# The gate of the pooling branch as a stage of its own by seven products

## The chip, the cores and the metric

The kernel runs on one core of one Trainium2 chip. The metric is the device time of one execution in microseconds. A core has a matrix engine (PE, with its weight loads shown as PEld), VectorE (DVE), ScalarE (ACT), GpSimd (POOL) and SyncE (SP, which here only issues transfers). Each engine takes its own instructions in order; they wait for one another by semaphores. PE writes its sums to eight banks of 512 floats per partition; here they are four tags ("pj", "z", "av", "tr") of two banks.

## The reference

One layer of a decoder block on a sequence of 1024 rows of width 1024, all in 32-bit floats. The input x is normed and modulated to h, and one projection of h gives eight parts of 1024 columns each:

```
h = rms_norm(x, norm_gain) * (1 + scale) + shift
q, k, v, z_a, u, z_b, m_a, m_b = split(h @ w_in)
attn   = stick_breaking(q, k, v)        # 16 heads of 64; A[t,s] = sigmoid(z_ts) * prod_{s<j<t} (1 - sigmoid(z_tj)), s < t
p_a    = (attn * silu(z_a)) @ w_branch_a
pooled = trailing-window means of u (2, 4, 8, 16) minus u, a linear map per group, a scale per channel
p_b    = (pooled * silu(z_b)) @ w_branch_b
merged = sigmoid(m_a) * p_a + sigmoid(m_b) * p_b
out    = final rms_norm(x + gate * (merged @ w_out))
```

The two joining gates are sigmoid(m_a) for the attention and sigmoid(m_b) for the pooling branch. Each comes from one 1024 x 1024 x 1024 product of h.

## The kernel before, in words

**Arithmetic.** A 32-bit operand is split into a high part (ScalarE rounds it, an fp32r number) and a low part (the rest, one subtraction on VectorE or GpSimd). A product takes three matmuls: high by high, high by low, low by high. So a tile of 128 columns of a projection, over eight blocks of 128 and two halves of the sequence, takes 48 matmuls of 128x512. h is held transposed, as `hT` (high and low), in SBUF. Time runs backwards along the sequence, which only matters to the order of rows.

**Stages, as us from the start of the span in the profile before.** Up to 128 the start (norm, `hT`, the weights of u with the pooling maps folded in, u). From 128 to 205 the values, from 205 to 300 the projection z_b with the pooling's window sums on VectorE, from 300 to 369 the branch p_b, from 369 to 1011 the attention, and to 1192 the finish (p_a and out).

**Seven products.** The values and p_b are computed by `seven` (L565): both 1024-wide operands are cut into four 512-blocks, sums and differences of blocks are formed (of the weights on VectorE as they are loaded, L576 to L588; of h once, in four tiles `ht0` to `ht3`, the list `tq`), and seven block products p1, p5, p6, p7, p4, p3, p2 of 48 matmuls each give the four blocks of the result: 336 matmuls in place of 384. Operands are loaded in halves ("quarters" of an operand, q = 0 and 1) by `raw`: the first of a pair goes to one of two buffers `raw`, the second to one of two buffers `ar`. `a_op` and `b_op` (L546, L552) make high and low parts of the two sides, on ScalarE and VectorE. After a product, `copied` (L598) takes sums out of PE's banks on ScalarE, `added` (L562) adds chains on VectorE, and `final` hands a finished 128x512 block to the caller: `values` rounds it (L683, ScalarE), subtracts (L684, VectorE) and stores both parts in `v_d` (L685, SP's queue). These stages keep all weight loads and these stores on the one queue of SP, in program order.

**Attention.** The heads are done in eight pairs, each pair in eight units of 256 query rows (`HT_ORDER`). For a unit: PE forms the scores z (L898 on), ScalarE the two sigmoids `om` and `be` (L907, L908), GpSimd masks the diagonal block (L912), VectorE scans `om` along the keys (L914) and multiplies `be` by it (L915). Then, a chunk of two key blocks at a time, PE transposes `be` into a bank (`wt`, tag "tr"), ScalarE rounds it (L933), VectorE subtracts the low part (L934) and PE multiplies by the values (`av`). Scores run three units ahead of the products (`LEAD`), turned chunks two ahead (`DEPTH`).

**The filler.** Between these pieces, PE is given quanta of three matmuls of the projections that are left: per pair the keys, the queries and the attention's gate z_a, and among them the tiles of the two joining gates, 40 tiles of 48 matmuls, 640 quanta. 62 quanta run ahead (`FIRST`), `QUANTA` = 70 in each pair, the remaining 18 behind the last pair. `GATES` says how many joining-gate tiles follow each pair's keys and queries; tiles left over go to the end. Keys and queries of a pair are projected during the pair before, made into high and low parts (`kh`, `klo`, `q`, `qlo`) and copied across partitions by transfers (`kh<-kh`). A filler tile's weights are loaded by SP (L129), rounded by ScalarE (L121) and subtracted by GpSimd (L116; one of the 40 by VectorE). A joining gate's half goes through a sigmoid on ScalarE (L167) and is stored from ScalarE's queue (L168) to `sa_d` or `sb_d`, which the finish reads back (L1074, L1076).

**What sets the order.** In the attention, PE's order is pinned to the order in which the program is written (`order`, L97); elsewhere, and on the other engines, a scheduler decides by its own estimate of when things are ready. On VectorE the multiplication by the scan is issued behind the next low part (`behind`, `flush`).

The functions that the change touches:

## Time and profile before

| what | value |
|---|---|
| median of 3 runs | 1191.57 us (1191.53 to 1192.69) |
| the profiled execution | 1194.0 us, its span 1192.3 us |
| mean granted clock of PE | 0.998 |
| PE busy | 1179.2 us (99%), 5650 instructions |
| VectorE busy | 826.6 us (69%) |
| ScalarE busy | 542.3 us (45%) |
| GpSimd busy | 255.1 us (21%) |
| attention, 369 to 1011 us | PE 639.1, VectorE 461.1, ScalarE 351.0, GpSimd 238.2 us |
| values, 128.4 to 205 us | PE 76.6, VectorE 49.9, ScalarE 36.6 us |
| matmuls of filler (p<-hT,w) | 1920 |

The span runs from the first to the last instruction of the profiled execution; the time of a run holds a little more than the span. A line of the timeline gives the start, the duration, the engine, the line, what is written and read, and in brackets the idle time before and what ended it; "SPq" and "ACTq" are the issuing of transfers by these engines. Busy time is an average over stages: what a change in one stage is worth is read in that stage.

### The profile page before, as it was taken

The numbers are of one execution on the slowest core, as the hardware profiler recorded it, in microseconds if no ns is written. First come the engines' busy times: TensorE is split into PE (matmuls) and PEld (weight loads), VectorE is DVE, ScalarE is ACT, GpSimd is POOL, SyncE is SP. The second block draws the span as 40 slices with busy tenths as digits, with TensorE's granted clock in tenths as the row PEclk, the third lists the DMA queues.
The fourth block names the chain that finished last, engine by engine and source line by source line (L and its number), as shares of the span: only waits on it lengthen the run. The fifth ranks groups of instructions, "written<-read, shape, count | busy, mean of one in ns | idle before, by whom it ended". The sixth has DMA issues, their size and how long they took to land.

```text
span 1192.3 us, 15804 instructions
## 1 busy us (share of the span) xinstructions
PE 1179.2 (99%) x5650; PEld 984.6 (83%) x5650; DVE 826.6 (69%) x1093; ACT 542.3 (45%) x1016; POOL 255.1 (21%) x384
## 2 busy tenths in 40 slices
PE   8999999999999999999999999999999999999997
PEld 7888888888888788888888888888888888888886
DVE  5767466698762577877778687786877853885643
ACT  5561354322541555556556565555555643232111
POOL 1000000000003233244333344333434431000001
PEclk9999999999999999999999999999999999999999
DMA  9652329653457331422415224152321224974612
GB/s 349 259 187 98 131 91 318 229 192 89 142 175 237 92 98 46 136 84 89 106 47 137 85 85 100 56 137 76 113 78 58 71 102 177 346 267 160 228 54 88
DMA packets 73312, 167.26 MB, mean 140 GB/s; under 512 B 9233, under 2 KB 22673, under 8 KB 71058
## 3 DMA queue, kind: packets, MB, share of 16 engines
q1 hardware_dynamic: 65026, 151.38, 39.2%
q10 hardware_dynamic: 8208, 14.88, 3.4%
q8 instruction: 44, 0.72, 0.3%
q14 instruction: 34, 0.28, 0.1%
HBM read 115.89 MB, written 33.56 MB: 125 GB/s over the span
## 4 chain that ended last, share of the span: by engine, by line
PE 82%; DVE 7%; DMA 5%; issue 4%; POOL 1%; ACT 1%; SPq 1%; POOLq 0%; ACTq 0%; DVEq 0%
PE p L101 33%; PE pa L101 7%; PE o L101 6%; PE vp L101 6%; PE z L101 5%; PE av L101 5%; PE wt L101 5%; PE u L101 5%; PE bp L101 4%; PE ua L101 3%; DMA u<-u_d 2%; PE wm L101 1%; DVE om L914 1%; DMA kh<-kh 1%; DVE gb L716 1%
## 5 line engine op out<-in xcount | busy, mean ns | idle before, releaser
L101 PE MATMUL p<-hT,w 128*128 128x512 f32 x1920 | 479.9, 391 | 0.0
L101 PEld LDWEIGHTS p<-hT,w 128*128 128x128 f32 x1920 | 355.2, 188 | 73.9 <-DVE klo L101 0.2
L914 DVE TENSOR_TENSOR_SCAN om<-om 128x512 f32<-128x512 f32 (+7 forms) x128 | 191.2, 1494 | 85.0 <-ACT om L907 51.9
L116 POOL TENSOR_TENSOR w<-w_raw,w 128x1024 fp32r<-128x1024 f32 x39 | 97.2, 2491 | 414.7 <-ACT w L121 409.7
L907 ACT ACTIVATE om<-z 128x512 f32<-128x512 f32 (+2 forms) x192 | 94.6, 493 | 157.1 <-PE z L101 134.6
L934 DVE TENSOR_TENSOR wt<-wt,wt 128x512 fp32r<-128x512 f32 (+1 forms) x160 | 99.4, 621 | 39.4 <-ACT wt L933 38.7
L912 POOL TENSOR_SCALAR_AFFINE_SELECT om<-om 128x128 f32<-128x128 f32 x128 | 72.7, 568 | 205.2 <-ACT om L907 201.8
L933 ACT CAST wt<-wt 128x512 fp32r<-128x512 f32 (+1 forms) x160 | 88.0, 550 | 49.4 <-PE wt L101 49.0
L101 PE MATMUL av<-wt,vv 128*128 128x512 f32 x320 | 106.3, 413 | 0.0
L101 DVE TENSOR_TENSOR be<-be,om 128x511 f32<-128x511 f32 (+7 forms) x128 | 101.1, 794 | 2.0 <-POOL be L912 0.7
L908 ACT ACTIVATE be<-z 128x512 f32<-128x512 f32 (+2 forms) x192 | 94.0, 490 | 0.0
L101 PE MATMUL wt<-ident,be 128*128 128x128 f32 x576 | 89.8, 273 | 1.8 <-DVE wt L934 1.8
L101 PE MATMUL pa<-ga,wa 128*128 128x512 f32 x384 | 89.6, 389 | 0.1
L101 PE MATMUL o<-wo,mhl 128*128 128x512 f32 (+1 forms) x408 | 89.6, 377 | 0.0
L101 PE MATMUL wzb<-hT,wzb 128*128 128x512 f32 x384 | 87.2, 389 | 0.0
L101 PEld LDWEIGHTS o<-wo,mhl 128*128 128x128 f32 x408 | 73.5, 188 | 14.1
L101 PEld LDWEIGHTS pa<-ga,wa 128*128 128x128 f32 x384 | 72.0, 188 | 15.4 <-DVE wa L116 0.5
L101 PEld LDWEIGHTS wzb<-hT,wzb 128*128 128x128 f32 x384 | 72.1, 188 | 14.9
L101 PEld LDWEIGHTS wt<-ident,be 128*128 128x128 f32 x576 | 69.8, 140 | 15.0 <-DVE wt L934 2.5
L101 PE MATMUL z<-kl,q 128*128 128x512 f32 (+2 forms) x192 | 65.5, 341 | 0.0
L101 PE MATMUL z<-kh,q 128*128 128x512 f32 (+2 forms) x192 | 64.0, 334 | 1.1 <-DMA q<-qlo 1.1
L101 PE MATMUL u<-hT,wg 128*128 128x512 f32 x240 | 55.5, 391 | 0.0
(217 smaller groups left out, 1482.0 us busy)
## 6 DMA issues: line engine op xcount, KB each, us to landing
w_raw<-in_w_in SPq DMA_DIRECT2D x40, 512.0 KB, 3.5
v_d<-vo SPq DMA_DIRECT2D x16, 512.0 KB, 4.1
vv<-v_d SPq DMA_DIRECT2D x8, 1024.0 KB, 5.6
wa_raw<-in_w_branch_a SPq DMA_DIRECT2D x16, 512.0 KB, 4.3
wa<-in_w_mod SPq DMA_DIRECT2D x7, 1024.0 KB, 7.5
kh<-kh SPq DMA_DIRECT2D x48, 128.0 KB, 2.3
va<-in_w_v SPq DMA_DIRECT2D x10, 512.0 KB, 3.6
ba<-in_w_branch_b SPq DMA_DIRECT2D x10, 512.0 KB, 4.2
```

What stands on the lines that cost most here:

```text
L101: ins = op(*args, **kw)
L116: lo_eng.tensor_tensor(lo, src, hi.bitcast(F32), op=ALU.subtract)
L716: v.scalar_tensor_tensor(z, dhls[j][:, sh * 512:sh * 512 + 512], psc_v[:, j:j + 1], z, ALU.mult, ALU.mult)
L907: act.activation(om[:, b0:b0 + n], zp[:, :n], AF.Sigmoid, scale=-0.125)
L908: act.activation(be[:, b0:b0 + n], zp[:, :n], AF.Sigmoid, scale=0.125)
L912: gp.affine_select(out=tl[:, :P], in_=tl[:, :P], pattern=[[1, P]], compare_op=ALU.is_gt, fill=fill, base=0, channel_multiplier=-1)
L914: v.tensor_tensor_scan(om[:, :W], om[:, :W], om[:, :W], 1.0, ALU.mult, ALU.min)
L933: act.copy(wt[:, 0, :off], pt[:, :off])
L934: v.tensor_sub(wt[:, 1, :off], pt[:, :off], wt[:, 0, :off].bitcast(F32))
```

## The change

The eight tiles of m_b leave the filler. They are computed by `seven("m", ...)`, behind the values and ahead of z_b, from the same four sums of h (`tq`), whose high and low parts are made again, and from the weights in blocks (`w_mb`, a copy of those columns of `w_in`, laid out like the values' weights). A finished block goes through the sigmoid on ScalarE into one of three buffers and is stored by SP (`gate_b`). The filler has 32 tiles, 512 quanta: 62 ahead, `QUANTA` = 55 in each pair, 10 behind. `GATES` now places one tile of m_a in every second pair; the other four stay for the end. The banks take turns differently: "av", "tr" for the chain b of the new stage, and the branch p_b has its two sets of banks exchanged, with z_b's turns starting afresh. `direct` says that the fourth block may be handed over in PE's bank; it had been tied to `a_moves`.

```diff
-QUANTA = (70,) * 8
-GATES = (0, 1, 2, 1, 2, 1, 1, 2)
+QUANTA = (55,) * 8
+GATES = (0, 1, 0, 1, 0, 1, 0, 1)
...
-    turns = [cycle(("av", "tr", "pj", "z")), cycle(("pj", "z", "av", "tr"))]
+    turns = [cycle(("av", "tr", "pj", "z"))]
...
-    gates = [c + j for j in range(KB) for c in (CMA, CMB)]
+    gates = [CMA + j for j in range(KB)]
...
-    def seven(nm, sums, load, b_of, a_moves, ta, tb, final):
+    def seven(nm, sums, load, b_of, a_moves, ta, tb, final, direct):
...
-                    final(1, 0, j, ps[j] if a_moves else copied("s3", 4, j + 4, ps[j]))
+                    final(1, 0, j, ps[j] if direct else copied("s3", 4, j + 4, ps[j]))
...
+        def h_parts(nm, pl):
+            def of(name, q):
                 if name in ("p1", "p2", "p3"):
                     k, n = dict(p1=(0, 0), p2=(1, 0), p3=(1, 1))[name]
                     return lambda m, e: hT[:, m, 4 * k + 2 * q + e, 512 * n:512 * n + 512]
+                return b_op(k2(tq[("p5", "p6", "p7", "p4").index(name)], q), pl, 2, f"{nm}{name}b{q}")
+            return of
...
-            seven("v", vs, load_v_w, h_parts, True, ("av", "tr"), ("pj", "z"), values)
-    turns.pop(0)
+            seven("v", vs, load_v_w, h_parts("v", vs), True, ("av", "tr"), ("pj", "z"), values, True)
+        with pool("ms", side="right") as ms:
+            def load_m_w(t, m, k, q):
+                nc.sync.dma_start(t.rearrange("p k c -> p (k c)"), a["w_mb"][m, 2 * k + q])
+            def gate_b(m, n, j, src):
+                t = ms.tile([P, 512], F32, tag="go", bufs=3, name=f"sb{4 * m + j}_{n}")
+                act.activation(t, src, AF.Sigmoid)
+                nc.sync.dma_start(sb_d[4 * m + j][:, 512 * n:512 * n + 512], t)
+            seven("m", ms, load_m_w, h_parts("m", ms), False, ("pj", "z"), ("av", "tr"), gate_b, True)
+    turns[0] = cycle(("av", "tr", "pj", "z"))
...
-    seven("b", sums, load_b_w, g_parts, False, ("pj", "z"), ("av", "tr"), branch)
+    seven("b", sums, load_b_w, g_parts, False, ("av", "tr"), ("pj", "z"), branch, False)
...
-            gates = [(c + j, j, d_) for j in range(KB) for c, d_ in ((CMA, sa_d), (CMB, sb_d))]
+            gates = [(CMA + j, j, sa_d) for j in range(KB)]
```

The diff doesn't show three places of the order. First SP's queue at the end of the values in the kernel before (`v_d<-vo` are the stores of finished values; `u`, `sg`, `gbias` and `wzb3_raw` belong to what follows them):

```order
L685 DMA v_d_75<-vo1_0_1633 128x4x256
L129 DMA wzb3_raw_1897<-in_w_in 128x1024
L685 DMA v_d_75<-vo2_0_1638 128x4x256
L685 DMA v_d_75<-vo3_0_1643 128x4x256
L703 DMA gbias_1659<-in_b_gate 128x8
L526 DMA u0_1662<-u_d_78 128x1024
L725 DMA sg_1661<-in_c_row 128x1024
```

In the changed kernel (`ma21`, `ma22`, `ma11s` are the new stage's blocks of weights for p5, the last number before the underscore is the half):

```order
L687 DMA v_d_75<-vo1_0_1633 128x4x256
L697 DMA ma21_1_1764<-in_w_mb 128x1024
L687 DMA v_d_75<-vo2_0_1638 128x4x256
L687 DMA v_d_75<-vo3_0_1643 128x4x256
L697 DMA ma22_0_1728<-in_w_mb 128x1024
L697 DMA ma11s_0_1731<-in_w_mb 128x1024
L697 DMA ma22_1_1766<-in_w_mb 128x1024
L697 DMA ma11s_1_1769<-in_w_mb 128x1024
```

The second operands of p5 stand directly behind the last two stores of values. ScalarE's order at the same place, in the changed kernel (`ms1` is a sum of p1 copied out of its bank, `mp5b` and `mp5a` the high parts of the two sides of p5):

```order
L685 CAST vo3_0_1643<-vs1_3_1157 128x8x64
L598 COPY ms1_0_1714<-mp1_0_1652 128x512
L554 CAST mp5b0_1737<-ht0_832 128x1024
L554 CAST mp5b1_1775<-ht0_832 128x1024
L598 COPY ms1_1_1716<-mp1_1_1653 128x512
L598 COPY ms1_2_1718<-mp1_2_1654 128x512
L598 COPY ms1_3_1720<-mp1_3_1655 128x512
L548 CAST mp5a0_1734<-ma21_0_1726 128x1024
```

All four copies of p1's sums stand ahead of the first high part of p5's left side. The kernel before has here the high parts of z_b's weights and z_b's activations (L715).

Then PE in the attention, at the turn from pair 5 to pair 6. The names are: `p30` and `p15` filler (the number is the tile), `z6_...` scores of pair 6, `wt5_...` and `wt6_...` turned chunks, `av5_...` products with the values; x9 stands for nine matmuls. Before:

```order
L101 MATMUL av5_1_1_7675<-wt5_1_1_1_7552,vv_5_6798 128x2x128
L101 MATMUL p15_0_7684<-hT_91,w15_29_7508 128x512 x9
L101 MATMUL wt5_1_3_3_7694<-ident_79,be5_1_6_7477 128x128 x2
L101 MATMUL wt5_1_3_3_7694<-ident_79,be5_1_7_7537 128x128
L101 MATMUL av5_1_1_7675<-wt5_1_1_2_7619,vv_5_6798 128x512 x2
L101 MATMUL p15_0_7684<-hT_91,w15_29_7508 128x512 x9
L101 MATMUL z6_0_5_0_7714<-kh_6_6971,q0_6_7138 128x384
L101 MATMUL z6_0_5_0_7714<-kl0_2829,q0_6_7138 128x384
L101 MATMUL wt6_0_0_0_7724<-ident_79,be6_0_0_7572 128x128 x2
```

The same place in the changed kernel:

```order
L101 MATMUL av5_1_1_7897<-wt5_1_1_1_7773,vv_5_7145 128x2x128
L101 MATMUL p30_1_7868<-hT_91,w30_23_7552 128x512 x6
L101 MATMUL wt5_1_3_3_7906<-ident_79,be5_1_6_7707 128x128 x2
L101 MATMUL wt5_1_3_3_7906<-ident_79,be5_1_7_7758 128x128
L101 MATMUL av5_1_1_7897<-wt5_1_1_2_7843,vv_5_7145 128x512 x2
L101 MATMUL p30_1_7868<-hT_91,w30_23_7552 128x512 x6
L101 MATMUL z6_0_5_0_7923<-kh_6_7325,q0_6_7555 128x384
L101 MATMUL z6_0_5_0_7923<-kl0_3376,q0_6_7555 128x384
L101 MATMUL wt6_0_0_0_7933<-ident_79,be6_0_0_7802 128x128 x2
```

The turned chunks and the scores keep their order; between them six filler matmuls stand where nine stood, and elsewhere three where six stood.

More of the change, by code (lines that the diff above doesn't have):

```diff
@@ L666, in block_kernel @@
         early.close()
+        def h_parts(nm, pl):
+            def of(name, q):
+                if name in ("p1", "p2", "p3"):
+                    k, n = dict(p1=(0, 0), p2=(1, 0), p3=(1, 1))[name]
+                    return lambda m, e: hT[:, m, 4 * k + 2 * q + e, 512 * n:512 * n + 512]
+                return b_op(k2(tq[("p5", "p6", "p7", "p4").index(name)], q), pl, 2, f"{nm}{name}b{q}")
+            return of
         with pool("vs", side="right") as vs:
@@ L671, in load_v_w @@
                 nc.sync.dma_start(t.rearrange("p k c -> p (k c)"), a["w_v"][m, 2 * k + q])
-            def h_parts(name, q):
-                if name in ("p1", "p2", "p3"):
-                    k, n = dict(p1=(0, 0), p2=(1, 0), p3=(1, 1))[name]
-                    return lambda m, e: hT[:, m, 4 * k + 2 * q + e, 512 * n:512 * n + 512]
-                return b_op(k2(tq[("p5", "p6", "p7", "p4").index(name)], q), vs, 2, f"v{name}b{q}")
             def values(m, n, j, src):
@@ L1159 @@
     w_v = np.asarray(w_in)[0][:, 2 * D:3 * D].reshape(4, 2, P, 2, 512).transpose(3, 0, 2, 1, 4)
+    w_mb = np.asarray(w_in)[0][:, CMB * P:CMB * P + D].reshape(4, 2, P, 2, 512).transpose(3, 0, 2, 1, 4)
     w_ut = np.asarray(w_in)[0][:, CU * P:CU * P + D].reshape(2, 512, 4, 2, P).transpose(2, 0, 4, 3, 1)
@@ L1178 @@
         "w_v": np.ascontiguousarray(w_v).reshape(2, 4, P, D),
+        "w_mb": np.ascontiguousarray(w_mb).reshape(2, 4, P, D),
         "pool_w": np.ascontiguousarray(np.asarray(pool_w)[0]),
```

## The prediction

> **What bounds the kernel now.** I read the page's engine totals first, then PE's waits, then the windows by stage, then the chain of waits. In the windows the columns are PE, PEld, DVE, ACT and POOL busy (with instruction counts), the granted clock, the DMA share and GB/s.
>
> ```profile
> PE 1179.2 (99%) x5650; PEld 984.6 (83%) x5650; DVE 826.6 (69%) x1093; ACT 542.3 (45%) x1016; POOL 255.1 (21%) x384
> ...
> PE wt L101 <- DVE wt L934: 1.8, 4, 0.5
> ...
> 128.40:205.00 76.60, 76.60 (x340) 63.45 (x339) 49.85 (x54) 36.55 (x49) 0.00 (x0) 1.00 0.58 188
> 369.00:1011.00 642.00, 639.08 (x3201) 536.38 (x3200) 461.10 (x603) 350.99 (x736) 238.24 (x330) 1.00 0.33 98
> ...
> 128.48 74.36 PE vp L101 x328
> 992.86 18.39 PE p L101 x81
> ```
>
> PE is busy for 1179.2 of 1192.3 us, and in the whole attention (369 to 1011) it waits for another engine four times, for VectorE's low part of a turned block, 1.8 us in all. So the time is the number of matmuls times their interval, as long as nothing else becomes late. The chain gives the interval: 74.36 / 328 = 0.2267 us in the seven products of the values, 18.39 / 81 = 0.2270 in the filler. The granted clock is 1.00 in both stretches.
>
> **The matmuls removed: −10.9 us.** The gate was 8 tiles of 48 = 384 matmuls of filler; as seven products of 48 it is 336 in a stage of its own. Both kinds are 128x512 at 0.2267: the attention loses 384 × 0.2267 = 87.1, the new stage adds 76.2. Of 640 quanta (three matmuls each) 512 remain: 62 ahead of the turns, 8 × 55 inside the pairs (8 × 70 before), 10 behind the last (18 before). This term holds only where PE keeps its pace; the next three ask where it doesn't.
>
> **The new stage's second product: +2.3 us (1.5 to 4).** The values' own stage ran 76.60 of 76.60 us, with VectorE at 49.85 and ScalarE at 36.55, so the same seven products on the same sums should run without a gap once fed. The question is the feeding at the join.
>
> ```profile
> 193.60 11.04 PE L101 MATMUL vp<-vp2a,hT 128*128 128x512 f32 x48
> 204.48 27.82 PE L101 MATMUL wzb<-hT,wzb 128*128 128x512 f32 x122
> ...
> 208.21 0.62 ACT L683 CAST vo<-vs 128x512 fp32r<-128x512 f32 x1 [1.91 <-DMA v_d<-vo]
> ...
> 208.86 0.69 DVE L684 TENSOR_TENSOR vo<-vs,vo 128x512 fp32r<-128x512 f32 x1 [1.17 <-ACT vo L683]
> ...
> 207.72 2.22 SPq L685 DMA_DIRECT2D v_d<-vo  x2
> ...
> 210.97 1.19 SPq L526 DMA_DIRECT2D u<-u_d  x1
> ...
> va<-in_w_v SPq DMA_DIRECT2D x10, 512.0 KB, 3.6
> ba<-in_w_branch_b SPq DMA_DIRECT2D x10, 512.0 KB, 4.2
> ...
> L598 ACT COPY vs<-vp 128x512 f32<-128x512 f32 x12 | 7.1, 589 | 8.1 <-PE vp L101 8.0
> L548 ACT CAST vp5a<-va 128x1024 fp32r<-128x1024 f32 x2 | 2.1, 1051 | 0.0
> ```
>
> The values' last product ends at 204.48; call it T. The last value row is rounded by ScalarE at 208.21 (it waited for a store to free its buffer) and subtracted at 208.86, and SP is held with its last two stores until 207.72 + 2.22 = 209.94 = T + 5.5. In the changed order the loads of a22 and a11, the first operands of the new p5, stand on SP right behind these two stores. They land 3.6 to 4.2 later, at T + 9.1 to 9.7; the add takes 1.25, so p5's left operand exists at T + 10.4 to 11. ScalarE's copy of p1's fourth sum now stands ahead of its rounding: p1 ends at T + 48 × 0.2267 = T + 10.9, then copy 0.59 and cast 1.05: p5 begins no earlier than T + 12.5, 1.6 after p1, and 1.2 more where it waits for the low part. That gives 1.6 to 2.8. The second half of p5's operands shares two buffers with the first and is loaded once the first add has freed one: T + 11 plus 4.2 for the load, 1.25, 1.05 and 1.2 for add, cast and low part is T + 18.7, and the first half's 24 matmuls end at T + 13.2 + 5.4 = T + 18.6. In the stage of the branch the same wait cost nothing, since its add came 1.6 after p5's start:
>
> ```profile
> 302.52 11.15 PE L101 MATMUL bp<-p5b,bp5a 128*128 128x512 f32 x48
> ...
> 304.14 1.23 DVE L576 TENSOR_TENSOR ba<-ba,ba 128x1024 f32<-128x1024 f32 x1 [2.01 <-DMA ba<-in_w_branch_b]
> ```
>
> So 1.5 to 4; I take 2.3, near the lower sum, because the low part is only the third matmul's operand and the second half comes about even. The stage's stores go onto SP's queue behind its loads: all loads but the last two products' are issued before the first store, and 18 loads of 512 KB in 76 us is what the values had (DMA share 0.58 there), so I cost them at nothing; if that cover failed, the next stage's operands would come late by one store's hold of SP, about 1.1 each.
>
> **Attention with less filler: +6.6 us (0 to 27).** This is the term that decides. A pair's filler falls from 210 to 165 matmuls, 10.2 us less PE work per pair, while VectorE's scans and low parts per pair stay. I cut out, in each pair from the second, the stretch in which VectorE has least room: from the start of a pair's first long scan to the low part of the turned block that PE needs before the second head's first row (chunk 1,0,2):
>
> ```profile
> 466.83:512.58 45.75, 45.32 (x232) 37.93 (x230) 40.05 (x47) 26.67 (x55) 16.46 (x23) 1.00 0.40 110
> 540.99:585.74 44.75, 44.75 (x230) 37.52 (x228) 39.07 (x47) 25.88 (x54) 20.04 (x23) 1.00 0.37 104
> 613.46:658.28 44.82, 44.82 (x228) 37.68 (x227) 40.44 (x48) 27.04 (x55) 16.13 (x23) 1.00 0.35 95
> 687.04:733.73 46.69, 46.69 (x238) 39.26 (x237) 41.12 (x47) 28.30 (x58) 20.39 (x25) 1.00 0.34 99
> 760.68:804.39 43.71, 43.71 (x222) 36.70 (x222) 38.78 (x47) 25.25 (x52) 16.95 (x23) 1.00 0.38 106
> 832.93:880.56 47.63, 46.80 (x236) 38.87 (x235) 40.89 (x47) 28.01 (x57) 19.31 (x25) 1.00 0.38 106
> 907.18:952.28 45.10, 45.02 (x228) 37.63 (x227) 38.44 (x44) 26.94 (x55) 19.84 (x23) 1.00 0.19 65
> sum 318.45, PE 317.11 PEld 265.59 DVE 278.78 ACT 188.08 POOL 129.12; mean PE 45.30 PEld 37.94 DVE 39.83 ACT 26.87 POOL 18.45
> ...
> 514.51 0.49 PE L101 MATMUL wt<-ident,be 128*128 128x128 f32 x3
> ...
> 954.51 0.49 PE L101 MATMUL wt<-ident,be 128*128 128x128 f32 x3
> ```
>
> Over seven stretches the mean is 318.45 / 7 = 45.5 long, VectorE busy 39.8 and idle 5.7. PE takes up the bank that the low part frees somewhat later; in the first and the last of the seven (the two rows of PE) 514.51 − 512.58 = 1.9 and 954.51 − 952.28 = 2.2, and the mean of the seven is 1.7. So PE has 47.2. In the order this stretch holds 138 filler matmuls before and 108 now: 30 × 0.2267 = 6.8 less, 40.4 left. VectorE's own work in it falls a little, since fewer weights' low parts run on GpSimd beside its scans:
>
> ```profile
> 489.58 2.40 POOL L116 TENSOR_TENSOR w<-w_raw,w 128x1024 fp32r<-128x1024 f32 x1 [2.09 <-ACT w L121]
> 489.99 3.87 DVE L914 TENSOR_TENSOR_SCAN om<-om 128x896 f32<-128x896 f32 x1
> ...
> 637.11 2.02 DVE L914 TENSOR_TENSOR_SCAN om<-om 128x896 f32<-128x896 f32 x1
> ```
>
> The same scan takes 2.02 alone and 3.87 beside a low part, 1.85 more. 38 such low parts fall into 642 us, 2.7 per stretch; of 30 some 2.1 will, so at most 0.6 × 1.85 = 1.1 less, and 0.2 for a klo or qlo that slides out: 38.5. That leaves 40.4 − 38.5 = 1.9 for VectorE's idle time where 5.7 stood. What of the 5.7 stays decides: all of it, (5.7 − 1.9) × 7 = 26.6; half, (2.85 − 1.9) × 7 = 6.6; a third or less, 0. What ends it, over the attention:
>
> ```profile
> L914 DVE TENSOR_TENSOR_SCAN om<-om 128x512 f32<-128x512 f32 (+7 forms) x128 | 191.2, 1494 | 85.0 <-ACT om L907 51.9 <-POOL om L912 31.6 <-issue 0.5
> L934 DVE TENSOR_TENSOR wt<-wt,wt 128x512 fp32r<-128x512 f32 (+1 forms) x160 | 99.4, 621 | 39.4 <-ACT wt L933 38.7
> ```
>
> Of 85.0 + 39.4 = 124.4 the 51.9 follow PE's scores, which now come earlier; the 31.6 and 38.7, 57%, are the length of a chain (mask, cast), which a VectorE that comes late finds partly done. I take half.
>
> In the Trainium skill, "SBUF — State Buffer", section "SBUF: two separate sides", VectorE and GpSimd share one port pair that is an exclusive lock for the whole instruction. The trace agrees: the scan beside the low part ended 1.9 us after it (493.86 against 491.98), its own length alone. Taken at its fullest, each of the eight low parts that leave had blocked VectorE for all its 2.40, once a pair instead of my 0.6 times 1.85; VectorE would need 37.2, and with half its idle time the stall would be nil.
>
> Two further deadlines. The keys and queries of the next pair are ready 6 quanta or more of PE work ahead where they were 18 or more, a margin that still covers ScalarE, VectorE and the 2.3 us of the copies; I cost it at nothing, and at 3 us a pair if a copy queues on SP. A filler tile has more time for its weights, (642.0 − 87.1) / 32 = 17.3 us against 642.0 / 40 = 16.1, so their supply is free.
>
> **The tail: +1.2 us (0 to 3).** Behind the last pair 30 filler matmuls remain where 54 of the 81 below stood, 5.4 us less cover for what the finish waits for:
>
> ```profile
> 992.70 18.55 PE L101 MATMUL p<-hT,w 128*128 128x512 f32 x81
> ...
> 1002.57 0.62 ACT L873 CAST ga<-gr 128x512 fp32r<-128x512 f32 x1 [7.01 <-DMA gr<-ga_d]
> ...
> 1003.59 1.04 ACT L121 CAST wa<-wa_raw 128x1024 fp32r<-128x1024 f32 x1
> ...
> 1004.66 1.23 DVE L116 TENSOR_TENSOR wa<-wa_raw,wa 128x1024 fp32r<-128x1024 f32 x1 [0.74 <-ACT wa L121]
> ...
> 1011.09 2.20 PE L101 MATMUL pa<-ga,wa 128*128 128x512 f32 x9
> ```
>
> The last pair's output goes to memory and back, its last cast starts 1002.57, the first finish weight is ready 1004.63 (high) and 1005.89 (low), and PE uses it at 1011.09: 5.2 to 6.5 of room. PE now arrives 5.4 earlier, so between 0.2 of room and 0.2 short by the high part, and a further 1 if ScalarE's remaining gate sigmoids stand before that cast; 1.2.
>
> **Sum:** −10.9 + 2.3 + 6.6 + 1.2 = −0.8. The profiled execution took 1194.0 us (span 1192.3), so 1193.2 for one like it; the median of the runs, 1191.57, is 2.4 shorter at the same work, and against it the sum gives 1190.8.
>
> **Rivals.**
>
> *The idle time gives way (faster).* If VectorE, once late, finds its inputs ready, the 5.7 us shrink to 1.9 and PE keeps its pace through the attention. Only the join and the tail are paid: −10.9 + 2.3 + 1.2 = −7.4, 1184.2. For it: PE waited 1.8 us in 642 so far, and the whole pair leaves room, VectorE's 461.1 / 8 = 57.6 a pair against PE's 62.5 (642.0 less the 62 quanta ahead, 42.2, and the 18.4 behind, by 8 is 72.7, less 10.2). Against it: in the stretch itself 38.5 of 40.4 is 95% busy, and VectorE's order is the scheduler's, with single waits that the average hides.
>
> *VectorE becomes the bound of the stretch (slower).* If 4.2 of the 5.7 us stay, since most of it is the chain from transposes over ScalarE's cast, each of the seven stretches ends (4.2 − 1.9) = 2.3 late, 16.1 in all: −7.4 + 16.1 = +8.7, 1200.3; with all of it kept 1210.8. It decides from the point where −7.4 is used up, 7.4 / 7 = 1.06 a stretch, an idle time of 2.95 us. For it: the four waits that PE has already are all of this kind, and the filler shrinks just where turned chunks follow each other, from nine matmuls to six. Against it: VectorE is busy in 39.83 / 45.5 = 88% of the stretch now, and each turned chunk had room enough for PE not to wait.
>
> *The new stage starves at its start.* If SP is held longer by the value stores, or the second half's loads come a further 4 us late, p5 costs 6 to 8 in place of 2.3 and, with the rest as forecast, the time is about 1195.5. For it: SP's next load behind the last two stores went out 6.5 us after T. Against it: the next product on PE is 10.9 us away from that point, and in the branch's stage a second half's add that came 1.6 after p5's start cost nothing.
>
> On this the Trainium skill, "TensorE: Matmul & The Clock Gate", section "Why this matters for your kernels", warns that a gap of PE above about 3 us brings its clock down to half. No run here shows such a gap between 128 and 1011 us (the granted clock is 1.00 in both windows above); an estimate from that page's window of about 3.4 us at half clock is 1.7 us more for this rival, 1197.2.
>
> **How the numbers follow.** A measurement of this kernel tells about 0.2%, 2.4 us, from no change: faster is below 1189.2, slower above 1194.0. The forecast (half the idle time stays, 1190.8, its own range 1186.5 to 1195.5) has 0.40: 0.27 of it inside the band, 0.08 below, 0.05 above. The idle time giving way has 0.31, all of it faster. VectorE as the bound has 0.21, all of it slower. The starved start has 0.08: 0.04 inside the band, 0.04 above. Faster 0.39, same 0.31, slower 0.30. The range takes in the second case down to a join of 1.5 and a tail of nothing (−10.9 + 1.5 = −9.4, 1182.2, cut to 1182.5) and the third up to 1201.
>
> **What would show it.** Right: no PE gap but one of 1.5 to 4 us before the new stage's p5; waits of PE on VectorE's L948 (L934 before: the low part of a turned block) rising from 1.8 us to about 7, most in the stretches above, with VectorE's idle time there near 2.9; PE's first finish matmul 0 to 3 us after the last filler one. The idle time giving way: those waits below 3 us, stretches near 40.4. VectorE as the bound: waits above 10, stretches near 43 and more, VectorE above 90% in them. The starved start: a gap above 5 us ahead of p5, or later ones in p6 to p2. The forecast is wrong if PE waits for something that no term names, a copy of keys or queries or a load of weights, or if the matmul count is not 48 lower.

## The result and the profile after

The changed kernel takes 1206.69 us (median of 4 runs, 1205.39 to 1211.63) against 1191.89 for the kernel before in the same comparison: ratio 1.0131, 95% interval 1.0102 to 1.0160. It is slower by 14.8 us; 1190.8 was forecast and the range ended at 1201. The profiled execution took 1206.08 us with a span of 1204.3, 12.0 longer than the span of before; the accounts below are of these two executions.

The changed kernel's totals from its page, then PE's waits, then its stage and its attention by windows (columns as before), then the chain of waits around the attention:

```profile
PE 1174.5 (98%) x5602; PEld 976.4 (81%) x5602; DVE 861.4 (72%) x1135; ACT 563.9 (47%) x1042; POOL 241.6 (20%) x376
```

```profile
PE wt L101 <- DVE wt L948: 8.7, 9, 1.8
PE mp L101 <- ACT mp5a L548: 3.9, 1, 3.9
PE wt L101 <- POOL tp L977: 2.2, 3, 1.1
PE wt L101 <- DVE be L101: 1.9, 4, 0.6
...
PE mp L101 <- DVE mp6b L555: 0.8, 1, 0.8
```

```profile
205.17:289.44 84.27, 79.57 (x337) 64.94 (x337) 45.44 (x46) 38.05 (x51) 0.00 (x0) 0.96 0.52 176
453.40:1023.19 569.79, 555.17 (x2817) 463.52 (x2817) 451.72 (x603) 334.56 (x712) 224.79 (x322) 1.00 0.33 97
```

```profile
376.48 76.92 PE bp L101 x336
...
1011.60 11.58 PE p L101 x51
1023.19 21.76 PE pa L101 x96
```

The 48 matmuls are gone (5602 instructions for 5650). The new stage took 84.27 us where 336 × 0.2267 = 76.2 were due: **+8.1**. The attention, from the last matmul of p_b to the first of p_a, took 569.79; before, 1011.25 − 369.01 = 642.24, less the 87.1 of the gate's tiles is 555.1: **+14.7**. Before the join 0.5 were lost, z_b and p_b took 0.4 less. 0.5 + 8.1 + 14.7 − 0.4 − 10.9 = 12.0, the whole difference of the spans. The tail cost nothing: p_a's first matmul follows the last filler at once (1011.60 + 11.58 = 1023.18).

**The join.** The timeline of the changed kernel there, for SP, ScalarE, VectorE and PE, and then the windows of p1 and p5:

```profile
208.25 1.25 SPq L687 DMA_DIRECT2D v_d<-vo  x2
209.55 1.28 SPq L697 DMA_DIRECT2D ma<-in_w_mb  x1
213.19 0.59 ACT L598 COPY ms<-mp 128x512 f32<-128x512 f32 x1 [4.80 <-PE mp L101]
213.68 2.00 ACT L554 CAST mp5b<-ht 128x1024 fp32r<-128x1024 f32 x2
...
214.76 2.36 DVE L555 TENSOR_TENSOR mp5b<-ht,mp5b 128x1024 fp32r<-128x1024 f32 x2 [5.65 <-ACT mp5b L554]
217.64 1.23 DVE L576 TENSOR_TENSOR ma<-ma,ma 128x1024 f32<-128x1024 f32 x1 [0.52 <-DMA ma<-in_w_mb]
218.90 1.04 ACT L548 CAST mp5a<-ma 128x1024 fp32r<-128x1024 f32 x1 [1.76 <-DVE ma L576]
...
205.01 11.04 PE L101 MATMUL mp<-hT,mp1a 128*128 128x512 f32 x48
220.00 13.95 PE L101 MATMUL mp<-mp5b,mp5a 128*128 128x512 f32 x48 [3.95 <-ACT mp5a L548]
...
235.61 10.31 PE L101 MATMUL mp<-mp6b,mp6a 128*128 128x512 f32 x44 [0.75 <-DVE mp6b L555]
```

```profile
205.00:220.00 15.00, 11.05 (x50) 8.83 (x48) 8.60 (x10) 7.18 (x10) 0.00 (x0) 0.97 0.75 251
220.00:234.00 14.00, 14.00 (x49) 11.33 (x50) 8.02 (x8) 3.06 (x4) 0.00 (x0) 0.79 0.65 222
```

The load of a22 (`ma22` in the order of SP, one of p5's second operands) leaves SP at 209.55, right behind two stores, as forecast; it is added at 217.64, 8.1 later, where the median landing of such loads was 3.6 to 4.2. VectorE was busy until 214.76 + 2.36 = 217.12 with the low parts of p5's right side, so the add came late for two reasons. PE then stood for 3.95 us, and p5's 48 matmuls took 13.95 in place of 11.04: in that window the granted clock is 0.79. Four matmuls into p6, PE stood for another 0.75, for a low part of p6's right side. So the late start of p5 and what followed it make 3.95 + 2.9 + 0.75 = 7.6 of the 8.1.

**The attention.** The same stretches as before the change (from a pair's first long scan to the low part of chunk 1,0,2), by windows; the first and the last of the seven and the sum:

```profile
546.81:589.98 43.17, 39.04 (x198) 31.85 (x196) 39.16 (x46) 25.11 (x53) 18.36 (x25) 1.00 0.26 79
...
937.67:977.15 39.48, 39.45 (x205) 33.12 (x204) 37.00 (x45) 26.04 (x55) 17.53 (x24) 1.00 0.14 48
sum 289.04, PE 276.74 PEld 229.76 DVE 263.78 ACT 183.98 POOL 122.51; mean PE 39.53 PEld 32.82 DVE 37.68 ACT 26.28 POOL 17.50
```

The stretch is 289.04 / 7 = 41.3 long where 40.4 was PE's room; VectorE is busy for 37.7 of it and idle for 3.6. PE stood still for 289.04 − 276.74 = 12.3 us in the seven.

Where in a pair does PE wait? Counting the transposes of the changed kernel gives each wait its chunk: 8.2 of the 12.9 us of waits at turned chunks lie in a pair's first unit, at the chunks (0,2,2) and (0,2,3) that are turned there; 2.3 lie in the seventh unit. The timeline of VectorE and PE at the first of these places, the turn into pair 1:

```profile
567.73 2.02 DVE L928 TENSOR_TENSOR_SCAN om<-om 128x896 f32<-128x896 f32 x1
569.79 0.42 DVE L974 TENSOR_TENSOR tp<-av,tp 64x256 f32<-64x256 f32 x1
570.24 0.69 DVE L948 TENSOR_TENSOR wt<-wt,wt 128x512 fp32r<-128x512 f32 x1
570.85 1.13 DVE L101 TENSOR_TENSOR be<-be,om 128x895 f32<-128x895 f32 x1
572.16 1.29 DVE L928 TENSOR_TENSOR_SCAN om<-om 128x512 f32<-128x512 f32 x1 [0.19 <-POOL om L926]
573.37 0.66 DVE L948 TENSOR_TENSOR wt<-wt,wt 128x512 fp32r<-128x512 f32 x1
...
571.08 0.52 PE L101 MATMUL wt<-ident,be 128*128 128x128 f32 x3 [0.39 <-POOL tp L977]
574.08 0.66 PE L101 MATMUL wt<-ident,be 128*128 128x128 f32 x4 [0.99 <-DVE wt L948]
```

VectorE pauses for 0.19 us only. The low part that frees a bank for PE (570.24, 573.37) stands in its queue behind the scans and the multiplication of the second head's first rows; PE needs one low part per chunk, about every 3 us here (571.08, 574.08), and VectorE has 2.4 us of row work between the two (570.93 to 573.37). The row of PE at 571.08 names GpSimd's `tp`, which ended last; the low part had ended at 570.93, so at this place the two came within 0.1 us of each other.

### The profile page after: what moved, and what is told of

Read it like the earlier page. It is cut to its first block, busy times and chain, and to the rows that moved or that the text cites. A ratio compares the mean times of both kernels' runs of the same rounds, so it can differ in the third digit from the quotient of the medians.

```text
span 1204.3 us, 15853 instructions
## 1 busy us (share of the span) xinstructions
PE 1174.5 (98%) x5602; PEld 976.4 (81%) x5602; DVE 861.4 (72%) x1135; ACT 563.9 (47%) x1042; POOL 241.6 (20%) x376
## 4 chain that ended last, share of the span: by engine, by line
PE 81%; DVE 7%; issue 4%; DMA 4%; ACT 2%; POOL 1%; SPq 0%; POOLq 0%; ACTq 0%; DVEq 0%
PE p L101 21%; PE wzb L101 7%; PE pa L101 7%; PE bp L101 6%; PE o L101 6%; PE vp L101 6%; PE mp L101 5%; PE u L101 5%; PE z L101 4%; PE av L101 4%; PE wt L101 4%; DVE om L928 3%; PE ua L101 3%; PE wm L101 1%; DVE be L101 1%
## 5 line engine op out<-in xcount | busy, mean ns | idle before, releaser
L101 PE MATMUL p<-hT,w 128*128 128x512 f32 x1536 | 392.6, 392 | 0.0
L101 PEld LDWEIGHTS p<-hT,w 128*128 128x128 f32 x1536 | 283.0, 188 | 58.0 <-DVE klo L101 0.3
L928 DVE TENSOR_TENSOR_SCAN om<-om 128x512 f32<-128x512 f32 (+7 forms) x128 | 183.6, 1435 | 52.6 <-POOL om L926 27.4
L116 POOL TENSOR_TENSOR w<-w_raw,w 128x1024 fp32r<-128x1024 f32 x31 | 80.5, 2596 | 458.7 <-ACT w L121 453.6
L921 ACT ACTIVATE om<-z 128x512 f32<-128x512 f32 (+2 forms) x192 | 94.8, 493 | 130.6 <-PE z L101 99.3
L926 POOL TENSOR_SCALAR_AFFINE_SELECT om<-om 128x128 f32<-128x128 f32 x128 | 78.5, 613 | 182.2 <-ACT om L921 162.3
L101 PEld LDWEIGHTS o<-wo,mhl 128*128 128x128 f32 x408 | 73.5, 188 | 14.1
```

Source lines behind the costliest of these rows:

```text
L101: ins = op(*args, **kw)
L116: lo_eng.tensor_tensor(lo, src, hi.bitcast(F32), op=ALU.subtract)
L921: act.activation(om[:, b0:b0 + n], zp[:, :n], AF.Sigmoid, scale=-0.125)
L926: gp.affine_select(out=tl[:, :P], in_=tl[:, :P], pattern=[[1, P]], compare_op=ALU.is_gt, fill=fill, base=0, channel_multiplier=-1)
L928: v.tensor_tensor_scan(om[:, :W], om[:, :W], om[:, :W], 1.0, ALU.mult, ALU.min)
```

## The experiments

All are compared with the kernel before on the same chip; times are medians. Executions of the changed kernel and of some variants scatter by up to 7 us (before: 1 to 2), so differences below 2 us are read with care. The kernel before took 1191.85 to 1192.34 beside them, so variants that ran on different chips can be compared to about half a microsecond.

**Stores on another queue.** The last four stores of values issued by ScalarE.

```diff
-                nc.sync.dma_start(
+                (act if (m, n) == (0, 0) else nc.sync).dma_start(
                     v_d[4 * m:4 * m + 4, :, sb].rearrange("n p c -> p n c"),
```

> The last four stores of values (the fourth block of the result) are issued by ScalarE instead of SyncE; nothing else differs from the changed kernel. Theory Q (SyncE's queue: the loads of p5's second operands went out behind these stores at 209.5 and landed 8.0 us later): the loads go out at about 205 to 207, p5 starts about 2 us after p1's end in place of 3.95, the gap is under 3 us, p5 runs its 48 matmuls in 11.0 us in place of 13.95, the new stage takes 78 to 80 us in place of 84.3, the whole is 4 to 6 us shorter than the changed kernel (about 1201). Rival B (the transfers themselves are slow there, because stores and loads share the engines): the loads land as late as before, the gap stays at 3 to 4 us and the whole within 1 us of 1206.7.

Measured 1205.87 (ratio 1.0114, 1.0099 to 1.0130). The timeline of this variant:

```profile
212.50 0.59 ACT L598 COPY ms<-mp 128x512 f32<-128x512 f32 x1 [3.99 <-PE mp L101]
212.99 2.00 ACT L554 CAST mp5b<-ht 128x1024 fp32r<-128x1024 f32 x2
...
216.35 1.22 DVE L576 TENSOR_TENSOR ma<-ma,ma 128x1024 f32<-128x1024 f32 x1
...
218.70 13.92 PE L101 MATMUL mp<-mp5b,mp5a 128*128 128x512 f32 x48 [3.29 <-ACT mp5a L548]
```

The load of a22 left 1.5 us earlier, counted from p1's start (3.0 us behind it in place of 4.5), and landed after 6.3 us in place of 8.0; the gap shrank by 0.7 only. The add now waits for nothing from memory: it stands on VectorE behind the low parts of p5's right side, whose high parts stand on ScalarE behind the first copy of p1's sums. So the queue of SP was not the cause, only the last of several waits; theory Q falls. The time and the gap are those of rival B, but not for its reason: the load came earlier than before, and PE waited all the same.

**One pool of buffers.** All of p5's operands were held until the values were done. What they share is the pool `ms`, opened where `vs` closes.

```diff
-        with pool("ms", side="right") as ms:
-
             def load_m_w(t, m, k, q):
...
-                t = ms.tile([P, 512], F32, tag="go", bufs=3, name=f"sb{4 * m + j}_{n}")
+                t = vs.tile([P, 512], F32, tag="go", bufs=3, name=f"sb{4 * m + j}_{n}")
...
-            seven("m", ms, load_m_w, h_parts("m", ms), False, ("pj", "z"), ("av", "tr"), gate_b, True)
+            seven("m", vs, load_m_w, h_parts("m", vs), False, ("pj", "z"), ("av", "tr"), gate_b, True)
```

> The changed kernel with the new stage in the values' own pool of buffers (vs) in place of a pool of its own (ms) that opens when that one closes. PE's order is the same. The high parts of p5's right side then stand on ScalarE ahead of the values' last rows, the loads of a22 and a11 on SyncE ahead of the values' last stores. Theory P (the new pool's buffers lie where the old pool's are, so everything of p5 is held until the values are done): p5 follows p1 with a gap under 1 us, PE's clock stays at full speed, the stage takes 76 to 78 us in place of 84.3, the whole is 6.5 to 8 us shorter than the changed kernel, 1198.5 to 1200.5. Rival (the wait is the length of the loads and of add, rounding and subtraction): the gap stays above 2.5 us and the whole above 1203.

Measured 1199.96 (ratio 1.0067, 1.0045 to 1.0088), 6.7 less. VectorE's first addition for p5 and PE in this variant, from its timeline, and then its stage as a window:

```profile
207.53 1.22 DVE L576 TENSOR_TENSOR ma<-ma,ma 128x1024 f32<-128x1024 f32 x1
...
206.73 11.04 PE L101 MATMUL mp<-hT,mp1a 128*128 128x512 f32 x48
217.61 11.04 PE L101 MATMUL mp<-mp5b,mp5a 128*128 128x512 f32 x48
```

```profile
206.90:283.06 76.16, 76.16 (x337) 63.08 (x337) 43.08 (x44) 36.40 (x49) 0.00 (x0) 1.00 0.53 181
```

The addition comes 0.8 us after p1's start, where it came 12.6 after it in the changed kernel. No gap, full clock, 76.16 us (76.2 to 77.6 in the other kernels with one pool, with stops of up to 1.1 in p6). Theory P holds: the join's 8.1 came from the border between two pools of buffers, not from the work of the stage.

**No low parts of the filler's weights.** The third matmul reads the high part again, so keys, queries and gates lose their third term.

```diff
-        return load_w(a["w_in"][tiles[i]], name, act, v if i == MASKED else gp)
+        raw = wts.tile([P, KB, P], F32, tag="raw", bufs=2, name=name + "_raw")
+        nc.sync.dma_start(raw.rearrange("p k c -> p (k c)"), a["w_in"][tiles[i]])
+        hl = wts.tile([P, 2, KB, P], F32R, tag="whl", bufs=2, name=name)
+        act.copy(hl[:, 0], raw)
+        return hl[:, 0], hl[:, 0]
```

> The changed kernel without the low parts of the filler's weights: the third matmul reads the high part again, so PE's work is the same, 31 subtractions on GpSimd and one on VectorE are left out, and keys, queries and gates are less exact. Theory G (a weight's low part on GpSimd holds up the masks queued behind it and stretches VectorE's scans beside it, so it makes most of the attention's 14 us of waiting): PE's waits in the attention fall from 14.4 to 5 us or less, the whole is 9 to 13 us shorter, 1194 to 1198. Theory V (VectorE's own scans, products and low parts fill the stretch): the waits fall only by the 1.1 us a pair that I had costed, to 8 or more, the whole is 4 to 6 us shorter, 1201 to 1203.

Measured 1194.04, 12.7 less. The attention took 558.2 in place of 569.8. PE's waits there, and then VectorE's two large groups (busy, mean ns, idle before) in this variant:

```profile
PE wt L101 <- DVE wt L952: 5.5, 7, 1.0
```

```profile
L932 DVE TENSOR_TENSOR_SCAN om<-om 128x512 f32<-128x512 f32 (+7 forms) x128 | 176.0, 1375 | 71.7 <-ACT om L925 37.1 <-POOL om L930 27.5 <-POOL be L930 5.0
L101 DVE TENSOR_TENSOR be<-be,om 128x511 f32<-128x511 f32 (+7 forms) x128 | 95.5, 751 | 0.1
```

and in the changed kernel:

```profile
L928 DVE TENSOR_TENSOR_SCAN om<-om 128x512 f32<-128x512 f32 (+7 forms) x128 | 183.6, 1435 | 52.6 <-POOL om L926 27.4 <-ACT om L921 20.1 <-POOL be L926 3.6
L101 DVE TENSOR_TENSOR be<-be,om 128x511 f32<-128x511 f32 (+7 forms) x128 | 101.1, 794 | 1.1
```

31 subtractions on GpSimd stretch VectorE's scans by 183.6 − 176.0 = 7.6 and its multiplications by 5.6, together 13.2 us, 0.43 each on the mean. The time fell by more than theory V allowed, as theory G said.

**A shorter multiplication.** Only the first 128 columns of `be` are multiplied; the rest is left unmultiplied.

```diff
-order(v.tensor_mul)(be[:, 1:W], be[:, 1:W], om[:, :W - 1])
+order(v.tensor_mul)(be[:, 1:P], be[:, 1:P], om[:, :P - 1])
```

> The changed kernel with the multiplication of be by the scan cut to its first 128 columns (the rest is left unmultiplied): same instructions, VectorE's multiply falls from 101 us to about 35, 8 us less VectorE work a pair; GpSimd's work is the same. Theory V: PE's waits in the attention fall from 14.4 to 3 us or less, the whole is 10 to 14 us shorter, 1193 to 1197. Theory G: the scans still start late behind the masks and are still stretched, so waits of 7 us or more stay, the whole is 4 to 7 us shorter, 1200 to 1203.

Measured 1191.69, 15.0 less. PE's waits, and then the group of the multiplication, in this variant:

```profile
PE wt L101 <- DVE wt L948: 2.9, 3, 1.8
```

```profile
L101 DVE TENSOR_TENSOR be<-be,om 128x127 f32<-128x127 f32 x128 | 40.2, 318 | 1.9 <-POOL be L926 0.7
```

61 us less of VectorE's work and the attention takes 555.6: all but half a microsecond of the 14.7 is gone, with GpSimd's 2.4 us subtractions all in place. Theory G's "7 us or more stay" falls. Both theories were half right: what is short is VectorE's time in the stretch, and GpSimd takes some of it.

**Low parts on VectorE.**

```diff
-        return load_w(a["w_in"][tiles[i]], name, act, v if i == MASKED else gp)
+        return load_w(a["w_in"][tiles[i]], name, act, v)
```

> The changed kernel with the low parts of the filler's weights made by VectorE (1.22 us each) in place of GpSimd (2.40): 31 more instructions, 38 us more VectorE work, and none of GpSimd's long ones. Theory G: the masks come in time and no scan is stretched, each low part on GpSimd cost VectorE up to 1.85, more than 1.22, so the whole is 2 us shorter or more. Theory V: 4.7 us more VectorE work a pair, three fifths of it in the tight stretch, 2.9 us a pair, so PE's waits rise by 15 to 22 us and the whole is 1220 to 1230.

Measured 1205.13, 1.6 less than the changed kernel; the attention took 567.7 in place of 569.8. The window of the attention:

```profile
455.50:1023.10 567.60, 554.19 (x2817) 463.71 (x2816) 468.19 (x633) 334.78 (x712) 155.95 (x292) 1.00 0.33 97
```

VectorE is busy for 468.2 in place of 451.7 and PE is no worse off. Its scans and multiplications take 175.4 and 95.2 us here, so what GpSimd took from them (13.2 us by the variant without low parts) is given back here as well, 14.1. That contradicts theory V's 15 to 22 us by far and is near theory G's 2 us: VectorE's busy time as such doesn't set the waiting. That the place of its low parts of turned blocks among its other work does is what the timeline above suggests. Why 16.5 us more work cost nothing isn't settled by these runs.

**Dealing the filler by unit.** The shares of a pair's filler, worked out from VectorE's work per unit.

```diff
-SHARE = (7,) * 8
-GATES = (0, 1, 0, 1, 0, 1, 0, 1)
+SHARE = (5, 8, 4, 8, 4, 10, 6, 10)
+GATES = (0, 0, 1, 0, 1, 0, 1, 1)
```

> The changed kernel with the filler of a pair dealt to its eight units as 5, 8, 4, 8, 4, 10, 6, 10 in place of equal shares (worked out so that PE's work of each unit follows VectorE's), and two of the attention's gate tiles later (0,0,1,0,1,0,1,1), so that keys and queries are still ahead of their use. Total work is the same on every engine. Theory S (VectorE has enough time per pair and too little in the tight stretch): PE's waits in the attention fall from 14.4 to 6 us or less and the whole is 7 to 12 us shorter, 1195 to 1200. Rival (VectorE, with what GpSimd takes from it, is the bound of the whole pair): the waits move but stay at 11 or more, the whole within 3 us of 1206.7.

Measured 1216.26, 9.6 more: a clear miss of both theories. PE waits 20 times for a low part in place of 9. The units that turn four or three chunks (the first, third and fifth) got the least filler, and PE's waits at turned chunks in these three rose from 10.6 to 18.5 us. The milder deal, 8, 8, 6, 6, 6, 6, 8, 8, made from the places of the waits:

> As the kernel with shares 5, 8, 4, 8, 4, 10, 6, 10, with the milder shares 8, 8, 6, 6, 6, 6, 8, 8 (chosen from where PE waited: filler is moved from units 2 to 5 to units 6, 7, 0 and 1). Theory S: waits in the attention of 8 us or less, 5 to 9 us shorter than the changed kernel. Rival: within 3 us of it.

Measured 1202.17, 4.5 less: just short of theory S's 5 to 9, and more than the rival's 3. The waits at turned chunks are 11.5 where theory S had 8 or less, so it is borne out in part. With one pool, the first deal:

> Both edits, one pool and the shares 5, 8, 4, 8, 4, 10, 6, 10. By theories P and S together 14 to 19 us shorter than the changed kernel, 1188 to 1193, which is the kernel before or a little below it; by the rivals no better than 1199.

Measured 1207.73: 8.5 below the same deal without it, so the pool's gain adds to whatever the attention does; theory S had promised 1193 or less.

**One addition per unit.** PE adds the products with the high and the low part in one set of columns; VectorE adds once in place of twice.

```diff
-                mm(
-                    avs[u][:, :, :n], vv[...], wt[:, :, o:o + n], ...
-                )
+                for w in range(2):
+                    mm(avs[u][:, :n], vv[...], wt[:, w, o:o + n], ...)
...
-            for i in range(2):
-                v.tensor_add(tp[r], av[0:64, i], tp[r])
+            v.tensor_add(tp[r], av[0:64, :256], tp[r])
```

> The changed kernel in which PE adds the products with a turned block's high and low part into the same columns of its bank (two matmuls of up to 256 columns in place of one of up to 512), so that a finished unit takes one addition on VectorE in place of two: 64 additions of 0.41 us, 26 us of VectorE's work in the attention (3.3 a pair), are gone, PE has 320 more matmuls of the same columns in all. Theory V (what VectorE has to do in the stretch is the bound; 61 us less of it took away all 14 us of waiting): a part of the waits goes, PE's waits fall from 14.4 to 6 to 10 us, the whole is 4 to 8 us shorter than the changed kernel, 1199 to 1203. Rival C (not the work but the length of the chain transposes, rounding, subtraction, bank free is the bound): the waits stay within 2 us and the whole is 0 to 3 us longer, for PE's added instructions.

> The kernel before with the single addition. There PE waits 1.8 us for VectorE in the whole attention, so by theory V nearly nothing is to be had: 1190 to 1193; longer, up to 1195, only if the 320 added matmuls cost PE time. If it is shorter by more than 3 us, VectorE bound the kernel before too, and the trace of before was misread.

Measured 1205.29 on the changed kernel and 1198.45 on the one before, above the 1195 that was the most expected. In the first PE's waits in the attention fell from 14.4 to 7.6 us, as theory V said and rival C did not, but the time stayed. The control shows why; chain of waits of the kernel before with one addition:

```profile
291.17 76.92 PE bp L101 x336
...
1015.62 21.76 PE pa L101 x96
```

Its attention is 1015.62 − 368.09 = 647.5 in place of 642.2, with shorter waits: two matmuls of up to 256 columns take about 0.02 us more than one of up to 512, 320 times. What VectorE gave, PE paid.

> The single addition together with the one pool of buffers for the two stages of seven products. The pool took 6.7 us off (1200.0); by theory V 4 to 8 more, 1192 to 1196; by rival C 1200 to 1203.

> One pool, the single addition and the mild shares 8, 8, 6, 6, 6, 6, 8, 8. The mild shares took 4.5 us off the changed kernel alone; with VectorE relieved less is left to take: 1189 to 1194 by theory V, the first that would be level with the kernel before or below it; by rival C 1196 to 1199.

Measured 1197.22 and 1195.86. The first is 2.7 below one pool alone, the second 1.4 below that: less than theory V said in both. PE pays for the single addition.

**The first unit.** The most filler where the waits were.

> One pool, and the filler of a pair dealt as 10, 6, 5, 5, 5, 7, 8, 9, with the gate tiles as 0,0,1,0,1,0,1,1. The most filler goes to the pair's first unit and the one before it, where the trace of the changed kernel has 8.2 of the 12.9 us that PE waits at turned chunks (0,2,2 and 0,2,3, behind the scans of the second head's first rows). Theory F (the wait is made at that one place, so filler there hides it): waits at the first unit fall under 4 us without new ones of the same size, the whole is 4 to 9 us below the one pool's 1200.0, 1191 to 1196. Rival (filler taken from units 1 to 4 opens waits there, as with 5, 8, 4, 8, 4, 10, 6, 10): 1197 to 1204.

> One pool and equal shares, with only the gate tiles moved to 0,0,1,0,1,0,1,1, which went with every change of the shares. If the shares did it, this is within 1.5 us of 1200.0; if the place of the gate tiles did it, it is 3 us or more below.

Measured 1194.91 (5.0 below one pool alone) and 1198.65 (1.3 below). The gate tiles' place had little part. In the first, no wait is left in a pair's first unit, but 5.6 us have come up in the third and 5.6 in the fifth, which gave filler: theory F is right on the place and wrong on the cure, the waits move where filler is taken. Where the 5.0 us came from the traces don't show: in the profiled executions the attention of the first variant is 569.9 long and that of one pool alone 568.5; its execution was shorter because the values began 3.0 us earlier (127.6 against 130.6).

The next variants make the filler's low parts on VectorE. In what was expected of them units are counted from 0, so units 2 and 4 are the third and the fifth.

> The same with the filler's low parts made by VectorE in place of GpSimd. On the changed kernel alone that took 1.6 off; with more filler at the first unit theory F gives about the same, 1190 to 1195; if the added 38 us of VectorE's work now fall on the units that lost filler, it is 2 or more longer than the kernel without it.

> One pool, low parts on VectorE, filler dealt as 9, 6, 6, 5, 6, 7, 8, 8: one share goes back from the first unit and the last to units 2 and 4, where 10, 6, 5, 5, 5, 7, 8, 9 opened new waits of 5.6 us each with GpSimd's low parts. If each unit has its own limit: waits of 5 us or less in all, 1188 to 1191, the first that is below the kernel before. If the waits only move from unit to unit: 1190 to 1194.

> The same with 9, 5, 7, 4, 7, 7, 8, 8: units 1 and 3, which turn two or three chunks, give one more share each to units 2 and 4. If each unit has its own limit, 1187 to 1191; if units 1 and 3 now wait, 1191 to 1195.

> The kernel before with all low parts of the filler on VectorE. There VectorE has room, so neither its 47 us more of work nor the end of the locks should tell: 1189 to 1193. If it is 3 us or more shorter, the kernel before had a cost there that PE's waits (1.8 us) don't show; if it is longer, its room was smaller than the waits say.

With the low parts on VectorE the same deal takes 1190.95 (ratio 0.9992, 0.9982 to 1.0002); 9, 5, 7, 4, 7, 7, 8, 8 takes 1190.88 (0.9989, 0.9980 to 0.9999); and 9, 6, 6, 5, 6, 7, 8, 8 takes **1186.85 (0.9957, 0.9942 to 0.9972)**, below both kernels and below the 1188 that was the least expected. PE's waits in this one, and then its attention as a window:

```profile
PE wt L101 <- DVE wt L946: 3.2, 8, 0.7
...
PE wt L101 <- DVE be L101: 1.2, 2, 0.6
```

```profile
444.91:1004.42 559.51, 553.66 (x2818) 464.12 (x2817) 468.45 (x633) 334.51 (x712) 145.10 (x292) 1.00 0.34 99
```

4.6 us of such waits are left of 12.9, and the attention lies 4.4 above the 555.1 that the matmuls need. The last control, the kernel before with its low parts on VectorE, measures 1192.12 (1.0001, 0.9992 to 1.0011): there the place of the low parts makes no difference to the time. The two deals that are 4 us apart differ by one share here and there; how far the best lies from 9, 6, 6, 5, 6, 7, 8, 8 was not tried, nor was an uneven deal on the kernel before, where 1.8 us of such waits were left to take.

## Why the prediction was wrong

*The matmuls removed, −10.9.* Right: 48 fewer, and with one pool the stage runs in 76.16, the 76.2 of the sum.

*The new stage's second product, +2.3 (1.5 to 4).* Measured 8.1. The places were right (the loads behind the last stores, the copies of p1's sums ahead of the rounding), and the gap, 3.95, is inside the step's range, at its upper end. Three things in the step failed. It took the median landing of 3.6 to 4.2 us for loads that leave in a burst: from 207.65 on SP issued two stores and three loads, 2.5 MB in all, while the window shows 251 GB/s at a DMA share of 0.75, and a22 landed after 8.0. It took p5's right side for ready, though its roundings stood behind p1's first copy. Each of the two alone holds the add to 12.1 us or more after p1's start, where the sum had the load landed at 9.1 to 9.7; behind both stands the border between the pools, which the step didn't see: with one pool neither is left. And it gave the gap no after-effect, which was left to the rival of the starved start: 2.9 us at a lower clock. In size that rival, with its 6 to 8 and a lower clock, was the nearest, and it had 0.08; its reason, SP held longer by the stores, was not the cause, by the first experiment.

On the after-effect, these are PE's rows of p5 and p6 in the variant with low parts on VectorE:

```profile
221.84 12.81 PE L101 MATMUL mp<-mp5b,mp5a 128*128 128x512 f32 x48 [3.98 <-ACT mp5a L548]
...
237.71 10.27 PE L101 MATMUL mp<-mp6b,mp6a 128*128 128x512 f32 x44 [2.16 <-DVE mp6b L555]
```

Eight kernels have the gap ahead of p5, all those with two pools. It is 3.29 to 3.98 us long, and p5 took 12.67 to 13.95 in place of 11.04 behind it. The loss doesn't follow the length: 2.9 us behind 3.29, 1.8 behind 3.98. Gaps of 1.67 to 2.21 us ahead of p6 cost nothing more in four of the eight (44 matmuls in 10.27 to 10.31); in a fifth, the one with the single addition, a gap of 1.90 was followed by 11.90, and why isn't known. The Trainium skill, "TensorE: Matmul & The Clock Gate", section "Why this matters for your kernels", draws its line for such gaps at about 3 us; these runs agree, but for that one gap. The estimate that the prediction drew from that page, 1.7 us, fits five of the eight (1.6 to 1.8); the changed kernel and two others lost 2.8 to 2.9.

*Attention with less filler, +6.6 (0 to 27).* Measured 14.7. VectorE's need was well sized (37.7 busy in the stretch, 38.5 forecast). Two things were off. The idle time that stays is 3.6 of 5.7, 63%, not half; the rows had said 57% for the part that is a chain's length, and the step went below them on an argument. And the step weighed the stretch as one balance of room and need: with the measured 37.7 and 3.6 it would still give (41.3 − 40.4) × 7 = 6.3. PE stood for 12.3 in these stretches, because it waits chunk by chunk: room that is left at the end of a stretch doesn't help a wait in its middle, and 8.2 of the 12.9 us of waits at turned chunks fell in one unit of the pair, where the low parts stand behind the second head's first scans. "VectorE becomes the bound of the stretch", with 16.1 us, was nearest in size, and its sign of waits above 10 us came true, but its stretches of 43 us did not; it had 0.21.

*GpSimd's low parts.* The step priced each lock at 1.85 us, from one scan, and took at most 1.1 us a stretch for those that leave. By the runs a lock takes 0.43 on the mean, 13.2 over the attention and 1.65 a pair; even so the attention is 11.5 shorter without them. The estimate drawn from the Trainium skill's page "SBUF — State Buffer", section "SBUF: two separate sides", with each lock at its full 2.40 and no stall left, did not come true: eight low parts fewer left 12.9 us of waits.

*Keys, queries and weights.* Right: PE's wait for q is 1.3 us in the changed kernel against 1.1. *The tail, +1.2.* Measured 0; the stores and the last pair's way through memory were done in time, though the last run of filler matmuls fell from 81 to 51, 6.8 us and not the 5.4 that were counted.

*The sum.* −10.9 + 8.1 + 14.7, with 0.1 from elsewhere, against −10.9 + 2.3 + 6.6 + 1.2. Both large terms erred to the same side, and each took a mean (of landings, of a stretch) where PE waits for single late instructions. In the join that is only part of it: the after-effect of the gap, 2.9, was not in the sum at all.

## What to carry to other kernels

Filler that covers a slower engine has a price when it is taken away: before moving work out of it, find the place in the period where the other engine is latest and ask for the room there, chunk by chunk, not over the period. A saving in a stage of its own is kept only if the stage is fed across its border; the pool of buffers opened where another closes held back p5's operands here, and sharing one pool gave 6.7 us. Both put right, together with the low parts' place, the change was worth 5 us, of the 10.9 that the matmuls promised.

## What the runs showed of the hardware

A gap of PE of 3.3 to 4.0 us was followed by matmuls that cost 1.6 to 2.9 us more in all, whatever its length within that range (granted clock 0.79 in the 14 us behind one of 3.95, 0.87 in the 12.7 us behind one of 3.98); gaps of 1.7 to 2.2 us cost nothing more in four kernels of five. GpSimd's subtraction of 128x1024 (2.40 us) took 0.43 us from VectorE on the mean of 31, though a scan that met one in full took 3.87 in place of 2.02. Cutting a matmul of up to 512 columns into two of up to 256 cost PE about 0.02 us.
